# Mixer B's 24 attention tiles worked off inside the pair projections, with the three groups joined beside mixer M's keys and values

## The chip, the cores and the metric

One core of a Trainium2 chip runs the whole kernel. The metric is device time in microseconds (us) for one execution. Before the change the median of three runs is 1144.53 us (1140.45 to 1144.83).

## The reference

The kernel computes one layer of a causal decoder block on `x` (1024 tokens x 1024 channels) with a memory of 256 tokens. RMSNorm of `x` gives `h`; one projection of `h` is cut into the inputs of three mixers and three merge gates.

```python
h = RMSNorm(x)
# mixer A: chunked causal spatial gating:   u * (w_s @ layer_norm(v))
# mixer B: 3 groups x 4 heads (width 64), window attention at dilations 1, 4, 16
scores = einsum('bnqhd,bnkhd->bnhqk', qb, kb) * hd ** -0.5
scores = where(valid, scores + bias, -1e30)
m = max(scores);  p = exp(scores - m);  den = sum(p);  o = p @ v
# the three groups are then joined per token by weights exp(m_g - max_g m_g) * den_g
# mixer M: 4 heads (width 128) over the 256 memory tokens, softmax, values
# each mixer's output * silu(z), projected to 1024, times a sigmoid gate, summed
out = x + W_o @ merged
```

The queries and keys of B and M are normalised and scaled by learned weights; the rest of the reference has no bearing on the change.

## The kernel before, in words

All products run on TensorE (PE) with fp32 split into a high and a low part: `mm3` (L162 to L165) issues three matmuls, high x high, low x high and high x low. The program goes through these stages, one after the other on PE.

1. Load and norm of `x`, then mixer M's queries (`proj_mq`).
2. The "natural" products (tiles `n`, six blocks): B's queries and keys and its values, and A's value, with tokens on the partitions. They are stored to DRAM as `scr_qk[g]`, `scr_v[g]`, `scr_av`.
3. The pair projections (tiles `t`, the loop over `pairs` in `with ... as pp_`): everything that stays with channels on the partitions, that is A's `u` and gate (6 pairs), M's gate (2), B's gate (1) and the merge gates (12). Each of the 21 pairs is 7 Strassen-like products, and each product is 12 matmuls of 128x128 by 128x512 into a PSUM tile of tag "pj". `take` hands out the prepared left factor of a product; the steps in `steps` that prepare it (load raw weights, add them on VectorE (DVE), cast and subtract into `wh`/`wl`) run up to six factors ahead. `combine_products` adds the products up on DVE, `finish` applies Tanh or Gelu on ScalarE (ACT), and GpSimd (POOL) stores the two halves. In pairs 0 and 1 the memory `mem` is also loaded, squared, summed (`np_mem`) and normalised into `mh`, `ml` (`mem_steps`).
4. The attention stage. `kv_m` computes M's keys (`pk`, 48 matmuls) and values (`pv`, 48). `att_b` gives the steps of one of B's 24 tiles of 128 queries: `load` (queries and keys as tile `nat`, values as tile `v`, from DRAM), `s0` (four transposes into `qkt`, L765, copied out by ACT), `s1` (scores `sc`, plain at L799 for groups 1 and 2, three products for group 0; then add bias and take the maximum on DVE, L810; negate it, L812; Exp on ACT, L815), `s2` (four transposes per key block into `pt`, L823, copied out at L824) and `s3` (`po`, L830, copied at L836 and stored to `oscr` by POOL at L837). A tile has one key block or two: 13 have one, 11 have two. `att_m` does the same for the 8 tiles of M (`qt_m`, `sc_m`, `pr_m`, `pt_m`, `po_m`, with steps on POOL), and `combine` joins the three groups of B for 128 tokens (L851 to L897): mostly small steps on DVE, one transpose `yt` on PE.
5. `gates_b` and `gates` (tiles `pp`): the projections of the mixers' outputs, times the gates `tg` and `merged` that are loaded from `scr_g`.
6. The out projection (tiles `po`, `ro`).

The order of stage 4 is written by hand. `schedule` lays the steps of the tiles out by the lags in `LAGS`, `MLAGS` and `CLAGS`. The first nine rows of B's plan go into `queue`, and `spread(32)` with `pump()` pops them between the matmul triples of `kv_m`. Then B's steps continue with M's from `MSTART` on, two of B's to one of M's, with six rows of the combines mixed in from `CSTART` on. What is left of the combines is put in `queue` and popped between the first matmuls of `gates_b`. Engines run their own instructions in program order; DMA issues of SP and POOL are also in order on their queue.

Of the kernel before, what the change touches and what calls it, by code (L numbers as in the profile page):

```python
# [35 lines left out]


LAGS = (0, 2, 4, 6, 7)
MLAGS = (0, 1, 2, 4, 6, 8)
CLAGS = (0, 1, 2, 4)  # L40
MSTART = 9
CSTART = 22
CLATE = 30
# [3 lines left out]
def hybrid_block(  # L47
# [155 lines left out]
    def normalize(xs, pt, wcol, dst, cw, name, **kw):  # L203


        kp = KT // (cw // P)
# [207 lines left out]
    def load_raw(src, odd, name):  # L414
        if not odd:
            return raw(src, 512, name)
        st = tp.tile([P, 512], F32, name=f"wr_{name}", tag="wr", bufs=4)
        nc.sync.dma_start(out=st, in_=src)
        return st

    def prep_pair(i):
        add_steps([prepare_left(lambda q: load_raw(w_t[i][:, q * 512:(q + 1) * 512], i % 2, f"t{i}{q}"),
                                lambda: tp.tile([P, 512], F32, name=f"s1_{i}", tag="s1"), ready(f"t{i}"))])

    def prep_natural(b):
        add_steps([prepare_left(lambda q, kh=kh: load_raw(w_n[b, kh][:, q * 512:(q + 1) * 512], (b + (q in (1, 2))) % 2,
                                                          f"n{b}{kh}{q}"),
                                lambda kh=kh: (npool if kh else tp).tile([P, 512], F32, name=f"s1_n{b}{kh}", tag="s1"),
                                ready(f"n{b}{kh}")) for kh in range(2)])

    def combine_products(q, acc, sl, sa, sab, sc_, add):
# [7 lines left out]
        elif q == 3:  # L439
            V.tensor_tensor(out=sc_[:, sl], in0=acc, in1=sab[:, sl], op=ALU.add)  # L440
        elif q == 4:
            V.tensor_tensor(out=sab[:, sl], in0=acc, in1=sab[:, sl], op=ALU.add)
            add(3, acc, sc_[:, sl])
        elif q == 5:
            add(2, acc, sc_[:, sl])
# [11 lines left out]
    scr_b = [dram.tile([P, 4 * PW], F32, name=f"scr_b{g}") for g in range(3)]  # L457

    with tc.tile_pool(name="npool", bufs=1, side="right") as npool:
# [56 lines left out]
        for b, targets in enumerate(naturals):  # L516
            o = [rpool.tile([P, 2, 1024], F32, name=f"on{b}{c}", tag="r") for c in range(2)]
            sa, sab, sc_ = (npool.tile([P, 1024], F32, name=f"ns{c}{b}", tag=f"s{c}") for c in ("a", "ab", "c"))
# [46 lines left out]
            for q in range(7):  # L565
                w = take(2)
                rh, rl = rights[q]
                for t in range(2):
# [14 lines left out]
                    combine_products(q, acc, sl, sa, sab, sc_, add)  # L583
# [26 lines left out]
    with tc.tile_pool(name="ppool", bufs=1, side="right") as pp_:  # L610
# [5 lines left out]
        def finish(kind, o, q, name):  # L616

            d = o[q // 2][:, 512 * (q % 2):512 * (q % 2) + 512]
# [7 lines left out]
            if kind[0] == "u" and q in (1, 2):  # L626
                h = slice(512 * (q == 1), 512 * (q == 1) + 512)
                V.scalar_tensor_tensor(out=o[0][:, h], in0=o[1][:, h], scalar=0.5, in1=o[0][:, h],
                                       op0=ALU.mult, op1=ALU.mult)
# [3 lines left out]
        def mem_load(c):  # L633
            xm[c] = pp_.tile([P, KT, P], F32, name=f"xm{c}", tag="o", bufs=3)
            nc.sync.dma_start(out=xm[c], in_=memT[:, c * S:(c + 1) * S].rearrange("p (k t) -> p k t", t=P))

        def mem_squares(c):
            sm[c] = squares([xm[c]], P, f"mem{c}", G)

        def mem_norm(c):  # L640
            cs = slice(c * P, (c + 1) * P)
            normalize([xm[c]], sum_squares(sm[c], P, f"mem{c}"), mw,
                      lambda k0, xv: [(mh[:, k0:k0 + 4, cs], ml[:, k0:k0 + 4, cs], xv)], P, f"mem{c}", tag="rs")

        mem_steps = {(0, 0): [lambda: mem_load(0)], (0, 2): [lambda: mem_squares(0)],
                     (0, 4): [lambda: mem_norm(0), lambda: mem_load(1)], (0, 6): [lambda: mem_squares(1)],
                     (1, 0): [lambda: mem_norm(1)]}
        pages.append(pp_)
        mh, ml = (rpool.tile([P, KT, MEM], F32R, name=f"m{c}", tag="r") for c in "hl")
        for i, kind in enumerate(pairs):  # L650
            o = [pp_.tile([P, S], F32, name=f"o{i}{c}", tag="o", bufs=3) for c in range(2)]
            sa, sab, sc_ = (pp_.tile([P, 512], F32, name=f"s{c}{i}", tag=f"s{c}") for c in ("a", "ab", "c"))
            quarter = lambda q: o[q // 2][:, 512 * (q % 2):512 * (q % 2) + 512]

            def add(q, psum, s):
                V.tensor_tensor(out=quarter(q), in0=psum, in1=s, op=ALU.add)
# [12 lines left out]
            dst = {"u": lambda: [scr_us[kind[1]]],  # L669
                   "m": lambda: [scr_zm[2 * kind[1] + c] for c in range(2)],  # L670
                   "b": lambda: [scr_zb[c] for c in range(2)],
                   "g": lambda: scr_g[kind[1]][kind[2]:kind[2] + 2]}[kind[0]]()
            for c, t in enumerate(dst):
                G.dma_start(out=t, in_=o[c])
# [11 lines left out]
    oscr = {g: dram.tile([S, 264], F32, name=f"oscr{g}") for g in (1, 2)}  # L686
    cring = []

    def cb_(j):

        if not cring:
            cring.extend(rpool.tile([P, 2, 3, 264], F32, name=f"cring{i}", tag="r") for i in range(2))
        return cring[j // 2 % 2][:, j % 2]


    queue = deque()

    pace = [0.0, 0.0]

    def spread(slots):  # L700

        pace[0], pace[1] = len(queue) / slots, 0.0

    def drain():
        while queue:
            queue.popleft()()

    def pump():
        pace[1] += pace[0]
        while pace[1] > 0.999 and queue:  # L710
            queue.popleft()()
            pace[1] -= 1.0

    def schedule(tiles, lags):

        stages = [f() for f in tiles]
        return [[stages[t - lags[q]][q] for q in range(len(lags) - 1, -1, -1) if 0 <= t - lags[q] < len(tiles)]
                for t in range(len(tiles) + lags[-1])]

    def stream(tiles, lags):  # L720
        for step in schedule(tiles, lags):
            queue.extend(step)

    def rows(ap, g, j):


        d = DIL[g]
        if d == 1:
            return ap[j * P:(j + 1) * P, :]
        if d == 4:  # L730
            r, b = divmod(j, 2)
            return ap[512 * b:512 * (b + 1), :].rearrange("(i r) c -> r i c", r=4)[r]
        return ap.rearrange("(i r) c -> r i c", r=8)[j]

    def load_bias(g):
        b = ap_.tile([P, 4, 256], F32, name=f"bias{g}", tag="bias")
        c0 = 0 if g < 2 else 128
        v = bass.AP(scr_b[g].tensor, scr_b[g].offset + 127 + c0, [[4 * PW - 1, P], [PW, 4], [1, 256 - c0]])
        G.dma_start(out=b[:, :, c0:256], in_=v)
        return b  # L740

    def att_b(u, j):

        g = u.g
        nm = f"{g}{j}"
        split3 = g == 0
        kc = (j % 4) * P
        prev = (g == 0 and j > 0) or (g == 1 and j % 2 == 1)
        nk = 2 if prev else 1
        W = nk * P  # L750
        c = Unit()

        def load():
            if j == 0:
                u.bias = load_bias(g)
            c.nat = ap_.tile([P, 512], F32, name=f"nat_{nm}", tag="nat", bufs=3)
            nc.sync.dma_start(out=c.nat, in_=rows(scr_qk[g], g, j))
# [669 lines left out]
```

## Time and profile before

| | before |
|---|---|
| median of 3 runs | 1144.53 us |
| the profiled execution, its own time | 1145.57 us |
| its span from the first to the last instruction | 1143.9 us |
| PE busy | 1104.9 us (97% of the span) |
| DVE busy | 827.1 us (72%) |
| ACT busy | 490.6 us (43%) |
| POOL busy | 223.1 us (20%) |
| mean granted clock of PE | 0.982 of 2.4 GHz |

The stages stand in the span like this: natural products from 72.3 to 315.4 us, pair projections from 315.4 to 721.9, attention stage from 721.9 to 894.3, gates to 1064, out projection to the end. PE's busy time counts a matmul until its modelled end, and matmuls overlap, so the distance between the starts of two instructions tells more of what an instruction costs than its own duration does.

### The profile page before, as it was taken

To read this page: it belongs to the slowest core of one execution; us is meant where nothing else is said; L and a number is where in the kernel's file an instruction comes from. 1 tells how busy PE (TensorE), PEld (TensorE's weight loads), DVE (VectorE), ACT (ScalarE), POOL (GpSimd) and SP (SyncE) were. 2 spreads that over 40 slices of the span, in tenths; PEclk is the share of its full clock that TensorE was granted. 3 is DMA by queue.
4 is the path that set the end of the run, shared out by engine and by line. 5 is a ranking of instruction groups with operands and counts; after the bars stand their busy time and mean duration, and the time that the engine had idled before them with its cause. 6 is when DMAs were issued, how large, how long until landed. Compare 5 with 4: busy or idle time off the path is not lost. (4 is left out here: it accounts for less than half of the span.)

```text
span 1143.9 us, 18163 instructions
## 1 busy us (share of the span) xinstructions
PE 1104.9 (97%) x6664; PEld 966.1 (84%) x6664; DVE 827.1 (72%) x1741; ACT 490.6 (43%) x1031; POOL 223.1 (20%) x232
## 2 busy tenths in 40 slices
PE   8999999999999999999999999899999899998998
PEld 7789999999987888888888888677889677887998
DVE  6999899846888878775666664355899758559873
ACT  6653243223255434343434343457786373223320
POOL 0000441220000000000000000012332136656232
PEclk9999999999999999999999999898999899999899
DMA  6322322464232222332333314636433685522422
GB/s 194 109 82 89 121 94 94 140 220 131 96 122 88 92 94 91 109 123 96 110 111 114 108 74 138 206 114 179 134 93 89 226 283 184 177 97 65 138 101 85
DMA packets 75244, 143.33 MB, mean 125 GB/s; under 512 B 7973, under 2 KB 26004, under 8 KB 75156
## 3 DMA queue, kind: packets, MB, share of 16 engines
q1 hardware_dynamic: 63172, 101.59, 28.3%
q0 software_dynamic: 10544, 38.10, 9.3%
q10 hardware_dynamic: 1440, 2.49, 0.6%
q8 instruction: 52, 0.85, 0.3%
q14 instruction: 36, 0.29, 0.1%
HBM read 101.57 MB, written 42.94 MB: 126 GB/s over the span
## 5 line engine op out<-in xcount | busy, mean ns | idle before, releaser
L163 PE MATMUL t<-th,wh_t 128*128 128x512 f32 x336 | 132.5, 394 | 0.0
L165 PE MATMUL t<-th,wl_t 128*128 128x512 f32 x336 | 131.7, 392 | 0.0
L164 PE MATMUL t<-tl,wh_t 128*128 128x512 f32 x336 | 130.7, 389 | 0.0
L163 PE MATMUL n<-wh_n,th 128*128 128x256 f32 x384 | 108.2, 282 | 0.0
L165 PE MATMUL n<-wh_n,tl 128*128 128x256 f32 x384 | 107.6, 280 | 0.0
L164 PE MATMUL n<-wl_n,th 128*128 128x256 f32 x384 | 107.6, 280 | 0.0
L163 PE MATMUL t<-HH,wh_t 128*128 128x512 f32 x252 | 98.6, 391 | 0.0
L165 PE MATMUL t<-HH,wl_t 128*128 128x512 f32 x252 | 98.4, 390 | 0.0
L164 PE MATMUL t<-HL,wh_t 128*128 128x512 f32 x252 | 98.1, 389 | 0.0
L163 PE MATMUL n<-wh_n,HH 128*128 128x256 f32 x288 | 82.0, 285 | 0.0
L164 PE MATMUL n<-wl_n,HH 128*128 128x256 f32 x288 | 81.5, 283 | 0.0
L165 PE MATMUL n<-wh_n,HL 128*128 128x256 f32 x288 | 81.5, 283 | 0.0
L141 ACT CAST wh_t<-ws_t 128x512 fp32r<-128x512 f32 x66 | 40.8, 621 | 86.4 <-PE t L164 73.2
L165 PEld LDWEIGHTS t<-th,wl_t 128*128 128x128 f32 x336 | 63.1, 188 | 14.8
L164 PEld LDWEIGHTS t<-tl,wh_t 128*128 128x128 f32 x336 | 63.1, 188 | 14.0
L163 PEld LDWEIGHTS n<-wh_n,th 128*128 128x128 f32 x384 | 73.3, 191 | 1.5 <-issue 0.9
L163 PEld LDWEIGHTS t<-th,wh_t 128*128 128x128 f32 x336 | 63.2, 188 | 12.8
L164 PEld LDWEIGHTS n<-wl_n,th 128*128 128x128 f32 x384 | 72.1, 188 | 0.2 <-issue 0.2
L165 PEld LDWEIGHTS n<-wh_n,tl 128*128 128x128 f32 x384 | 72.2, 188 | 0.0
L141 ACT CAST wh_t<-wr_t 128x512 fp32r<-128x512 f32 x60 | 37.0, 621 | 77.5 <-PE t L164 70.5
L536 POOL TENSOR_TENSOR on<-on,nss 128x1024 f32<-128x1024 f32 x12 | 26.3, 2207 | 174.4 <-DVE nss L138 117.5
L165 PEld LDWEIGHTS t<-HH,wl_t 128*128 128x128 f32 x252 | 47.3, 188 | 10.4
(378 smaller groups left out, 3052.8 us busy)
## 6 DMA issues: line engine op xcount, KB each, us to landing
scr_g<-o POOLq DMA_DIRECT2D x24, 512.0 KB, 2.9
ws_t<-in_w_t SPq DMA_DIRECT2D x44, 256.0 KB, 3.0
wr_t<-in_w_t SPq DMA_DIRECT2D x40, 256.0 KB, 3.2
tg<-scr_g SPq DMA_DIRECT2D x16, 512.0 KB, 4.0
ws_n<-in_w_n SPq DMA_DIRECT2D x24, 256.0 KB, 3.1
wr_n<-in_w_n SPq DMA_DIRECT2D x24, 256.0 KB, 3.2
scr_qk<-on POOLq DMA_DIRECT2D x12, 512.0 KB, 4.4
nat<-scr_qk SPq DMA_DIRECT2D x24, 256.0 KB, 3.3
```

The costliest lines, as they stand in the source:

```text
L141: A.copy(out=hi, in_=y)
L163: T.matmul(o, lhsT=ah, rhs=bh, start=first, stop=False)
L164: T.matmul(o, lhsT=ah, rhs=bl, start=False, stop=False)
L165: T.matmul(o, lhsT=al, rhs=bh, start=False, stop=last)
L536: G.tensor_tensor(out=v, in0=v, in1=ss[:, 16 * ORD[q]:16 * ORD[q] + 16].unsqueeze(2) .to_broadcast([P, 16, 64]), op=ALU.mult)
```

## The change

- B's 24 tiles move from stage 4 into the pair projections. `start_b` writes their steps into `queue` (98 entries: `first`, `s2`, `s1`, `last` for each tile, in the order of groups 2, 1, 0), and `spread(7*(PAIRS-2)-1)` spreads them over 132 products: `pump()` after each product pops 0.74 of a step on average. `drain()` stands after the last pair.
- The tiles' buffers come from elsewhere: keys (`bk`), bias and `nat` (both in `bx`) from the ring of big tiles `rpool`, `pr` and `pT` from the rings of prepared weights `wh` and `wl` (9 each), scores from PSUM tag "sc" (2 banks) in place of "pj". All copies `pT` and `ob` are ACT's. The factors are prepared 5 ahead in place of 6.
- All three groups' outputs go to `oscr` in DRAM (24 stores in place of 16), and a combine loads three pieces in place of two.
- The pair stage gives up a buffer (`sc_`), its output tiles are 512 wide with a store for each, and some raw weights of odd pairs use other buffers.
- The memory's load, squares and norm move from pairs 0 and 1 to pairs 19 and 20, with 32 matmuls of the squares' sums in place of 16.
- Stage 4 has `kv_m` with the combines in `queue` (`spread(40)`: 32 slots in `kv_m`, the rest after the rows of M's plan), then M's 8 tiles by themselves. Nothing of the attention is left for `gates_b`'s queue if the 40 slots take it all.

```diff
+        for t in range(n + 1):
+            queue.append(lambda t=t: first(t))
+            if t:
+                queue.append(lambda t=t: tiles[t - 1].s2())
+            if t < n:
+                queue.append(lambda t=t: tiles[t].s1())
+            queue.append(lambda t=t: last(t))
...
+        start_b()
+        spread(7 * (PAIRS - 2) - 1)
         for i, kind in enumerate(pairs):
...
-                (lh, ll), = take(1)
+                (lh, ll), = take(1, 5)
...
-                combine_products(q, acc, slice(0, 512), sa, sab, sc_, add)
+                combine_products(q, acc, slice(0, 512), sa, sab, add)
+                pump()
                 for f in mem_steps.get((i, q), ()):
                     f()
...
+        mem_steps = {(PAIRS - 2, 4): [lambda: mem_load(0)], (PAIRS - 2, 6): [lambda: mem_squares(0)],
+                     (PAIRS - 1, 1): [lambda: mem_norm(0)], (PAIRS - 1, 2): [lambda: mem_load(1)],
+                     (PAIRS - 1, 4): [lambda: mem_squares(1)], (PAIRS - 1, 6): [lambda: mem_norm(1)]}
...
     rsqrt(mss, 32, 1.0 / 128)
-    bs = schedule([(lambda g=g, j=j: att_b(ug[g], j)) for g in (2, 1, 0) for j in range(8)], LAGS)
-    for t in range(MSTART):
-        queue.extend(bs[t])
-    spread(32)
+    stream([(lambda j=j: combine(j)) for j in range(8)], CLAGS)
+    spread(40)
     kv_m()
...
+    for step in schedule([(lambda j=j: att_m(j)) for j in range(8)], MLAGS):
+        for f in step:
             f()
+        pump()
     spread(12)
```

The rows below are the program's instructions in the order of one engine, out<-in and shape. The first place is PE in the first pair, between the second product (`t_1`) and the fourth (`t_3`). Before:

```order
L164 MATMUL t_1_3822<-HL,wh_t_2_3601 128x512
L165 MATMUL t_1_3822<-HH,wl_t_2_3602 128x512
L163 MATMUL t_2_3841<-th_117,wh_t_6_3675 128x512
L164 MATMUL t_2_3841<-tl_121,wh_t_6_3675 128x512
L165 MATMUL t_2_3841<-th_117,wl_t_6_3676 128x512
...
L163 MATMUL t_3_3864<-th_118,wh_t_7_3679 128x512
```

And now:

```order
L159 MATMUL t_1_3805<-HH,wl_t_2_3599 128x512
L524 MATMUL qkt_3821<-ident,bx 128x128 x4
L157 MATMUL t_2_3843<-th_117,wh_t_6_3672 128x512
L158 MATMUL t_2_3843<-tl_121,wh_t_6_3672 128x512
...
L159 MATMUL t_2_3843<-th_117,wl_t_6_3673 128x512
L554 MATMUL sc_3861<-bk_3775,qh_3826 128x128
L554 MATMUL sc_3862<-bk_3775,qh_3826 128x128
L554 MATMUL sc_3861<-bk_3775,qh_3826 128x128
L554 MATMUL sc_3862<-bk_3775,qh_3826 128x128
L157 MATMUL t_3_3881<-th_118,wh_t_7_3676 128x512
```

The first tile's transposes (`qkt`) and scores (`sc`) now stand between whole products of 12 matmuls, one product apart.

The second place is ACT at the same point of the first pair: `wh_t` are the casts of weights, `o` the activations of a finished quarter, `sa` a copied product. Before:

```order
L434 COPY sa_3782<-t_0_3793 128x512
L141 CAST wh_t_7_3926<-wr_t_3818 128x512
L623 ACTIVATE o_3780<-o_3780 128x512
L186 ACTIVATE xq_mem_3855<-xm_3807 128x512
L186 ACTIVATE xq_mem_3857<-xm_3807 128x512
L141 CAST wh_t_5_3948<-s_1_3878 128x512
```

And now:

```order
L537 ACTIVATE qh_3826<-qkt_3821,wq_87 128x256
L803 ACTIVATE o_3818<-o_3818 128x512
L538 ACTIVATE bk_3775<-qkt_3821,colt 128x2x128
L135 CAST wh_t_1_3877<-wr_t_3835 128x512
L570 ACT_TABLE_LOAD
L570 ACTIVATE pr_3857,ob_3859<-pr_3857,ng_3860 128x128 x2
L570 ACTIVATE pr_3858,ob_3859<-pr_3858,ng_3860 128x128 x2
L135 CAST wh_t_2_3895<-wr_t_3837 128x512
L135 CAST wh_t_6_3924<-wr_t_3835 128x512
```

The tile's copies and its four Exp (L570, line 815 before) stand among the casts of weights, behind a load of a function table; over the whole program ACT has 23 such loads where it had 9.

The third place is SP's queue of loads beside the products of M's keys and values: `ws_kvv` are the raw weights of the values, `cb` and `cring` the pieces for a combine. Before:

```order
L146 DMA ws_kvv_7312<-in_w_kv 128x512
L146 DMA ws_kvv_7318<-in_w_kv 128x512
L757 DMA nat_7120<-scr_qk_652 128x512
L759 DMA v_7122<-scr_v_655 128x256
L757 DMA nat_7127<-scr_qk_652 128x512
```

And now:

```order
L140 DMA ws_kvv_8660<-in_w_kv 128x512
L1090 DMA merged_9496<-scr_g_679 128x512
L1090 DMA merged_9497<-scr_g_680 128x512
L888 DMA cb_8487<-oscr_702 128x264
L891 DMA cb_8487<-oscr_703 128x1x264
L892 DMA cb_8487<-oscr_704 128x1x264
...
L892 DMA cb_8544<-oscr_704 128x1x264
L140 DMA ws_kvv_8666<-in_w_kv 128x512
```

Nine pieces for the first three combines and five loads of gates (`merged`) now stand ahead of the last five of M's eight value weights; the loads of B's `nat` and `v` are gone from here.

## Rows read from the trace of the kernel before

**Rows 1.** Busy time by stretch: from:to, us, PE, PEld, DVE, ACT, POOL, clock, DMA share, GB/s.

```profile
315.40:721.90 406.50, 405.63 (x1783) 333.01 (x1782) 278.77 (x470) 171.72 (x269) 22.06 (x38) 1.00 0.31 105
721.90:767.00 45.10, 40.83 (x205) 31.23 (x204) 20.30 (x85) 22.05 (x67) 5.25 (x7) 0.85 0.52 165
721.90:894.30 172.40, 158.91 (x1186) 137.31 (x1185) 125.33 (x507) 118.32 (x395) 44.37 (x53) 0.93 0.45 135
894.30:904.60 10.30, 6.44 (x34) 5.08 (x32) 7.27 (x22) 3.13 (x9) 0.76 (x1) 0.95 0.61 177
904.60:990.00 85.40, 81.51 (x416) 66.12 (x417) 58.10 (x80) 35.44 (x79) 40.33 (x28) 0.97 0.73 238
```

**Rows 2.** Timeline of PE in 721.9 to 767: start us, us, instruction, out<-in, count.

```profile
750.52 0.60 PE L765 MATMUL qkt<-ident,nat 128*128 128x128 f32 x4
...
751.19 0.40 PE L164 MATMUL pv<-wl_kvv,mh 128*128 128x512 f32 x1
...
752.35 1.00 PE L830 MATMUL po<-v,pT 128*128 128x64 f32 x8
...
753.48 0.39 PE L164 MATMUL pv<-wl_kvv,mh 128*128 128x512 f32 x1
...
754.65 0.60 PE L823 MATMUL pt<-ident,pr 128*128 128x128 f32 x4
...
755.33 0.39 PE L164 MATMUL pv<-wl_kvv,mh 128*128 128x512 f32 x1
755.56 0.40 PE L165 MATMUL pv<-wh_kvv,ml 128*128 128x512 f32 x1
...
756.87 0.39 PE L164 MATMUL pv<-wl_kvv,mh 128*128 128x512 f32 x1
```

**Rows 3.** Timeline of PE where tiles of group 0 run, two key blocks each.

```profile
821.00 1.04 PE L823 MATMUL pt<-ident,pr 128*128 128x128 f32 x8
821.97 0.39 PE L163 MATMUL sc<-kh,qh 64*128 64x256 f32 x2
...
822.88 0.66 PE L765 MATMUL qkt<-ident,nat 128*128 128x128 f32 x4
...
826.44 1.90 PE L830 MATMUL po<-v,pT 128*128 128x64 f32 x16
828.18 0.61 PE L823 MATMUL pt<-ident,pr 128*128 128x128 f32 x4
```

**Rows 4.** Busy time of one tile's instructions by engine, 721.9 to 894.3: `pr`, `ob`, `qkt`, `pt`.

```profile
721.90:894.30 172.40, 21.59 (x140) 16.84 (x140) 29.92 (x96) 44.80 (x192) 0.93 0.45 135
721.90:894.30 172.40, 25.54 (x168) 9.02 (x16) 0.93 0.45 135
721.90:894.30 172.40, 17.80 (x96) 11.97 (x96) 7.22 (x16) 20.20 (x48) 0.93 0.45 135
721.90:894.30 172.40, 21.59 (x140) 16.84 (x140) 8.23 (x12) 12.77 (x23) 0.93 0.45 135
```

**Rows 5.** Groups of instructions on ACT: loads of function tables, mean ns.

```profile
L613 ACT ACT_TABLE_LOAD x2 | 2.6, 1283 | 3.6 <-DVE o L656 3.6
```

**Rows 6.** Busy time of the tile `sc_m` on PE, PEld, DVE and ACT, 721.9 to 894.3.

```profile
721.90:894.30 172.40, 15.15 (x96) 13.15 (x96) 10.68 (x16) 15.75 (x64) 0.93 0.45 135
```

**Rows 7.** Timeline of PE at the end of M's tiles and the start of the gates.

```profile
890.80 3.74 PE L1008 MATMUL po_m<-pT_m,mv 128*128 128x128 f32 x32
894.29 0.48 PE L163 MATMUL pp<-yb0h,wh_p 128*128 128x512 f32 x1
...
904.57 0.77 PE L163 MATMUL pp<-yb0h,wh_p 128*128 128x512 f32 x1 [3.86 <-DVE merged L1097]
...
910.60 0.39 PE L165 MATMUL pp<-yb0h,wl_p 128*128 128x512 f32 x1
```

**Rows 8.** Waits of PE in 721.9 to 912: waited for, us, times, longest.

```profile
PE pp L163 <- DVE merged L1097: 3.9, 1, 3.9
...
PE pt L823 <- ACT pr L815: 2.0, 1, 2.0
```

More of the change, by code (lines that the diff above doesn't have):

```diff
@@ L457, in hybrid_block, with spread, drain, pump @@
     scr_b = [dram.tile([P, 4 * PW], F32, name=f"scr_b{g}") for g in range(3)]
+    oscr = [dram.tile([S, 264], F32, name=f"oscr{g}") for g in range(3)]
+    queue = deque()
+    pace = [0.0, 0.0]
+    def spread(slots):
+        pace[0], pace[1] = len(queue) / slots, 0.0
+    def drain():
+        while queue:
+            queue.popleft()()
+    def pump():
+        pace[1] += pace[0]
+        while pace[1] > 0.999 and queue:
+            queue.popleft()()
+            pace[1] -= 1.0
+    def schedule(tiles, lags):
+        stages = [f() for f in tiles]
+        return [[stages[t - lags[q]][q] for q in range(len(lags) - 1, -1, -1) if 0 <= t - lags[q] < len(tiles)]
+                for t in range(len(tiles) + lags[-1])]
@@ new lines, in hybrid_block, with keys, start_b, first @@
+    mb = Unit()
+    def keys(g):
+        k = rpool.tile([P, 2, 2, 512], F32R, name=f"bk{g}", tag="r")
+        mb.kh, mb.kl = k[:, 0], k[:, 1]
+    def start_b():
+        keys(2)
+        bx = rpool.tile([P, 4, 512], F32, name="bx", tag="r")
+        mb.bias = bx[:, 0:2, :].rearrange("p a (b t) -> p (a b) t", t=256)
+        mb.nat = bx[:, 2:4, :]
+        tiles = []
+        for g in (2, 1, 0):
+            u = Unit()
+            u.g, u.v = g, []
+            tiles += [att_b(u, j) for j in range(8)]
+        n = len(tiles)
+        tiles[0].load_bias()
+        tiles[0].load_nat()
+        tiles[0].load_v()
+        def first(t):
+            if t == 16:
+                keys(0)
+            if t < n:
+                tiles[t].s0()
+            if t + 1 < n:
+                tiles[t + 1].load_nat()
+        def last(t):
+            if t + 1 < n and (t + 1) % 8 == 0:
+                tiles[t + 1].load_bias()
+            if t:
+                tiles[t - 1].s3()
+            if t + 1 < n:
+                tiles[t + 1].load_v()
+        for t in range(n + 1):
+            queue.append(lambda t=t: first(t))
+            if t:
+                queue.append(lambda t=t: tiles[t - 1].s2())
+            if t < n:
+                queue.append(lambda t=t: tiles[t].s1())
+            queue.append(lambda t=t: last(t))
@@ L637, in mem_squares @@
+            for k in range(2):
+                nc.sync.dma_start(out=xm[c][k], in_=memT[:, c * S + 512 * k:c * S + 512 * k + 512]
+                                  .rearrange("p (k t) -> p k t", t=P))
         def mem_squares(c):
[L638 removed]
+            sm[c] = squares(xm[c], P, f"mem{c}", V, 0)
         def mem_norm(c):
+            if not mem:
+                mem.extend(rpool.tile([P, KT, MEM], F32R, name=f"m{c}", tag="r") for c in "hl")
             cs = slice(c * P, (c + 1) * P)
[L642 to L643 removed]
@@ L665, in hybrid_block @@
                     mm3(acc, lh[:, c], ll[:, c], rh[:, kk, :], rl[:, kk, :], kk == 0, kk == 3)
-                combine_products(q, acc, slice(0, 512), sa, sab, sc_, add)
+                combine_products(q, acc, slice(0, 512), sa, sab, add)
+                pump()
                 for f in mem_steps.get((i, q), ()):
                     f()
[L669 to L674, printed above, removed]
+        drain()
+        mh, ml = mem
         pages.pop()
@@ L685, in hybrid_block @@
     ap_ = att.enter_context(tc.tile_pool(name="att", bufs=2, side="right"))
[L686 to L733, printed above, removed]
```

278 lines of the change are left out of this document (133 added, 145 removed).

## The prediction, made before the changed kernel ran

> **What bounds the kernel now.** I read three views in this order: the busy time by stretch, PE's timeline inside the stretches, and PE's waits. In the first the reader should compare two rows [rows 1]. The pair projections take 406.5 us, and PE is busy 405.63 of them at a granted clock of 1.00: nothing is late there, the stage is as long as its matmuls. DVE is busy 278.8 us of it, ACT 171.7, POOL 22. The attention stage from 721.9 to 894.3 is another case: 172.4 us, a clock of 0.93, and DVE and ACT at 73% and 69%. There every tile is a chain over three engines, and PE waits or runs slowly between the links. So the change takes work out of a stretch where it is badly packed and puts it into one whose only limit is PE, and which has time left on DVE and ACT. A step there costs what it adds to PE's queue and no more, as long as its inputs are ready.
>
> **Part 1: 24 tiles between the products.** The price of a step between 128x512 matmuls can be read where the kernel already does it, among M's value products [rows 2]. Two matmuls without anything between them start 0.23 us apart (755.33, 755.56). From the start of a step to the start of the second matmul behind it, less one such pitch, I get: `qkt` 750.52 to 751.19, 0.44; `po` 752.35 to 753.48, 0.90; `pt` 754.65 to 755.33, 0.45; `sc` 755.56 to 756.87 less two pitches, 0.85. One tile with one key block: 2.64 us. With two key blocks I take the tile of group 0 [rows 3]: `pt` 0.97 (821.00 to 821.97), `sc` 0.91, `po` 1.74 (826.44 to 828.18), and `qkt` 0.44 as before, and 0.1 for the pitch that is lost behind a step: 4.2 us. Of the 13 single-block tiles one is split in three products and I count it with the dear ones: 12 x 2.64 + 12 x 4.2 = **82 us**. The steps' own durations would give more, but they overlap.
>
> Is the cover there? DVE gets the additions with the maximum (29.9 us, tile `pr`), the small steps on `ob` (up to 25.5, of which the copies go to ACT) and the low parts (7.2): at most 63 us. ACT gets the Exp (44.8), the copies of `qkt` (20.2), 35 copies of `pt` at 12.77 / 23 = 0.56 (19.4) and 24 copies of `po`, which I put at 10: 94 us [rows 4]. (In the row of `ob` the two columns are DVE and POOL.) Over 488 us of stage that makes DVE (279 + 63) / 488 = 70% and ACT (172 + 94 + 18) / 488 = 58%. The 18 us are 14 more loads of function tables, Exp against Gelu, at 1.283 us [rows 5]. None of it ends a product later unless it comes in a heap. From a tile's scores to its `pt` there are three steps, some four products or 11 us of PE; a tile's Exp chain is 4 to 6 us by the same rows.
>
> The Trainium skill, page "ScalarE: Activation LUTs", section "What ACT_TABLE_LOAD costs", puts each switch at about 2.66 us, because a drain of 1.38 us stands beside the load, and the page's rule is to batch calls by table set, which this change breaks. By that figure ACT would have 37 us in place of 18, an estimate that leaves it at 62%; no row here shows the drain.
>
> The loads `nat`, `v` and the bias and the 24 stores have their data long before they are wanted, and the stores of the pair stage double in number at half the size; SP and POOL have little else to do there. I cost them at nothing; POOL's 22 us are the cover. The memory's norm in pairs 19 and 20 is moved, and costs 16 more small matmuls: 16 x 0.11 (a quarter of a `pt`) = 1.8 us. So the last product ends at 721.9 + 82 + 1.8 = **805.7**, bounds 800 (single steps cheaper than their distance) and 815 (some 0.4 us of wait for each tile).
>
> **Part 2: what is left of the attention stage.** M's keys and values are 96 x 0.23 = 22.1 us on PE, and 24 transposes for `kt` and `yt` are 2.6: 24.7. They can't run that fast. The norm of the memory's second half now ends with the last product and not 380 us before it: Sqrt with a table load, a reciprocal and the split into `mh`, `ml`, about 2 us before the first `pk`. And SP now has the nine pieces of the combines and five gate loads ahead of the last five value weights. Some 5.6 MB must come in this time (weights 1.3 to 2.6, gates 1.3 to 1.8, pieces 1.2 to 2), and at the 238 GB/s of the busiest stretch [rows 1] that is 24 us. Loads and matmuls would each take 24 to 25 us; in sequence for a part of the way I take 34, with the 2 us 36.
>
> M's eight tiles then stand alone. A tile costs PE 0.45 for `qt_m`, 0.97 for two `pt_m`, at most 15.15 / 8 = 1.9 for `sc_m` [rows 6] and (894.29 - 890.80) / 2 = 1.75 for `po_m` [rows 7]: 5.1, or 40 us for all. No other tile fills PE in the first and last steps of the plan, where one tile's chain runs through ACT, DVE and POOL: 6 us more, three hand-overs of 2 us, the size of the wait for `pr` [rows 8]. 46, and 2 for the combines in it: **48 us**. The gates would start at 805.7 + 36 + 48 = 889.7, bounds 876 (kv 27, M 43) and 905 (kv 42, M 57). They started at 894.3: **-4.6**.
>
> **Part 3: the gates.** The first projections (`pp`) ran from 894.29, then PE waited 3.86 us at 904.57 for `merged`, and the next 14 matmuls took 6.03 us, 0.43 each in place of 0.23, which is the lower of the clock's two levels, 1.2 GHz: 2.8 us lost [rows 7, 8]. With 0.8 for the transposes between them that is 7.5 us that need not come again, since the first gates are now loaded before M's tiles and no combine is left. I take **-5**, because A's part behind them can wait for DVE as before; bounds 0 and -7.5.
>
> **Sum.** -4.6 - 5 = -9.6 on the profiled execution's 1145.57 us: 1136. The median of the runs is 1.0 lower than that execution, so **1135 us**. The out projection and the rest of the gates are untouched.
>
> **Rivals.** (a) *The gain is lost in M's stage.* 82 us of matmuls that were mixed with M's are gone from it; M's 5 us bursts stand between chains. For it: the stretch 721.9 to 767, where PE waited for B's first loads, has a clock of 0.85, and after the one wait of 3.86 us PE ran at 1.2 GHz [rows 1, 7]. If half of M's 40 us ran at that level, 40 x 0.5 = 20 us would be at half speed, so 10 more than in the sum: 1145, no change. Against it: M's DVE and ACT parts are smaller than its PE part, so PE may keep busy. The Trainium skill, page "TensorE: Matmul & The Clock Gate", section "HAM oscillation — how this bites in real kernels", tells of bursts of matmuls with waits between them that fall back to the lower clock each time; the trace agrees, with the 14 matmuls at 0.43 us. 0.22.
>
> (b) *Slower: PE waits at each tile's steps in the pair stage.* The place is PE's queue at `pt` (and `po`), which waits for Exp, which is in order on ACT behind casts of weights, table loads and what DVE brings late. PE's queue is in order too: behind a late `pt` stands the next product. One such wait was 2.0 us in the old stage [rows 8]. It decides from 15 us in all, 0.63 us for each tile; at 1 us a tile the kernel takes 1135 + 24 = 1159. Against it: four products lie between scores and `pt`, and PE's idle time in the stage was 0.9 us of 406.5 [rows 1]. 0.12; with other late links (the tail's loads) I give the slower side 0.14.
>
> (c) *The tail packs well*: kv 30, M 44, all of part 3: 805.7 + 74 = 879.7, -14.6 - 7.5 = -22: 1123. Half of that gain, 1128, is the more probable end. 0.19.
>
> (d) *The steps don't go where the text says*, the scheduler moving them behind the pairs: the order of PE shows `qkt` and `sc` between the first products, so I give it nothing.
>
> **Chances.** The forecast 0.45, (a) 0.22, (b) and its like 0.14, (c) 0.19. A measurement of this kernel can tell about 0.5%, 5.7 us, from no change. Faster than 1138.8: nearly all of (c), and 0.85 of the forecast, and a little of (a): 0.58. Within: the rest of the forecast and most of (a): 0.27. Slower than 1150.3: 0.15. The range leaves out the far half of (b) and the far end of (c): 1124 to 1150.
>
> **What would show it.** Right: the pair stage 406 + 84 = about 490 us with PE above 98% busy and a clock of 1.00, DVE near 70%; the first `pp` near 890; no wait for `merged`. Step by step: the distance from product to product with a `po` between 0.9 or 1.8 longer; `pk` starting 2 us after the last product; M's part 44 to 50 us. Wrong: idle PE before `pt` in the pair stage that names ACT (b), a clock below 0.9 in M's part (a), or PE waiting for `wl_kvv` for more than 12 us.

## The result and the profile after

The changed kernel takes 1156.66 us (median of 4 runs, 1154.61 to 1159.64), the kernel before beside it 1142.49 (4 runs). The ratio is 1.013, with a 95% interval of 1.0089 to 1.017: slower by 1.3%, clear of noise, where 1135 and a range of 1124 to 1150 were forecast. The table sets the two profiled executions side by side, by the starts of the first instruction of a tile on PE.

| stage | before, us | after, us | difference | forecast |
|---|---|---|---|---|
| start to the first `n` | 72.5 | 73.1 | +0.6 | 0 |
| natural products | 243.0 | 247.5 | **+4.4** | 0 |
| first `t` to the last product | 406.2 | 488.4 | +82.2 | +83.8 |
| last product to the first `pk` | 0.2 | 1.9 | +1.7 | +2 |
| the tail: first `pk` to the first `pp` | 172.3 | 96.9 | **-75.4** | -90.3 |
| first `pp` to the last `pp` | 156.4 | 152.7 | -3.7 | -5 |
| out projection | 88.9 | 88.9 | 0 | 0 |
| PE's last instruction to the end | 4.3 | 8.1 | **+3.8** | 0 |
| span | 1143.9 | 1157.6 | +13.7 | -9.6 |

The busy time by stretch of the kernel after has the columns of [rows 1]:

```profile
73.10:320.60 247.50, 245.01 (x2028) 240.91 (x2027) 193.70 (x378) 79.33 (x131) 50.26 (x49) 0.99 0.37 123
320.60:809.20 488.60, 488.60 (x2535) 402.14 (x2534) 309.28 (x712) 265.88 (x576) 53.78 (x98) 1.00 0.35 114
809.20:907.80 98.60, 76.10 (x456) 64.66 (x455) 84.98 (x239) 51.44 (x142) 35.01 (x35) 0.88 0.59 182
...
810.90:825.00 14.10, 12.51 (x52) 9.03 (x51) 8.89 (x22) 7.74 (x12) 0.54 (x1) 1.00 0.86 277
825.00:845.00 20.00, 13.98 (x54) 10.12 (x53) 17.76 (x72) 5.15 (x12) 4.28 (x6) 0.91 0.86 265
845.00:870.00 25.00, 14.66 (x78) 12.26 (x78) 24.00 (x66) 8.57 (x23) 13.03 (x13) 0.71 0.74 229
870.00:890.00 20.00, 18.21 (x133) 17.31 (x134) 19.23 (x47) 15.89 (x52) 10.38 (x10) 0.85 0.14 40
```

Read the second row first. With 24 tiles among its products PE is busy in all of the pair stage, at full clock, and DVE is at 309 / 489 = 63%, ACT at 54%. The third row is another kind of stretch: PE 77% and clock 0.88. Its cut into pieces says who holds it: from 825 to 890 DVE is busy 61.0 of 65 us, and from 845 to 870 it has 1 us free while PE has 10. The forecast counted this stage in loads and matmuls; the engine with the least to spare in it is DVE.

The price of a step in the pair stage can be read where the forecast read it in [rows 2], on PE's timeline of the kernel after:

```profile
480.76 0.40 PE L159 MATMUL t<-HH,wl_t 128*128 128x512 f32 x1
481.00 0.60 PE L578 MATMUL pt<-ident,pr 128*128 128x128 f32 x4
481.35 0.48 PE L157 MATMUL t<-HH,wh_t 128*128 128x512 f32 x1
481.67 0.39 PE L158 MATMUL t<-HL,wh_t 128*128 128x512 f32 x1
...
843.21 0.39 PE L159 MATMUL pv<-wh_kvv,ml 128*128 128x512 f32 x1
846.10 0.66 PE L959 MATMUL kt<-ident,knat 128*128 128x128 f32 x4 [2.50 <-POOL knat L978]
848.06 0.41 PE L925 MATMUL yt<-ident,cb 128*128 128x128 f32 x2 [1.31 <-issue]
848.84 1.09 PE L959 MATMUL kt<-ident,knat 128*128 128x128 f32 x4 [0.37 <-DVE mx L901]
854.36 0.66 PE L925 MATMUL yt<-ident,cb 128*128 128x128 f32 x2 [4.43 <-DVE mx L907]
854.82 1.49 PE L1003 MATMUL qt_m<-ident,mnat 128*128 128x128 f32 x6
```

A `pt` costs 481.67 - 481.00 - 0.23 = 0.44 us, against 0.45 forecast. The second half of the fence is the place where PE stood longest in the tail. The last value product starts at 843.21 and M's first step, `qt_m`, at 854.82: 11.6 us with 12 transposes of 128x128 in it. The longest wait is not for anything of M's. It is that of a combine's transpose `yt`, which stands ahead of `qt_m` in PE's order and waits 4.43 us for DVE. DVE's timeline of the same us shows why:

```profile
844.54 1.79 DVE L916 TENSOR_TENSOR cb<-cb,ew 128x256 f32<-128x256 f32 x2
846.25 1.26 DVE L919 TENSOR_TENSOR cb<-cb 128x256 f32<-128x256 f32 x1
...
847.54 0.42 DVE L920 TENSOR_TENSOR cb<-cb 128x256 f32<-128x256 f32 x1
...
847.95 0.74 DVE L963 SCALAR_TENSOR_TENSOR mkl<-kt,colt,mkh 128x512 fp32r<-128x512 f32 x1
...
849.81 1.20 DVE L136 TENSOR_TENSOR yb0l<-cb,yb0h 128x256 fp32r<-128x256 f32 x1
...
851.01 0.74 DVE L963 SCALAR_TENSOR_TENSOR mkl<-kt,colt,mkh 128x512 fp32r<-128x512 f32 x1
851.68 0.78 DVE L916 TENSOR_TENSOR cb<-cb,ew 128x256 f32<-128x256 f32 x2
852.38 0.41 DVE L919 TENSOR_TENSOR cb<-cb 128x256 f32<-128x256 f32 x1
...
852.83 1.28 DVE L920 TENSOR_TENSOR cb<-cb 128x256 f32<-128x256 f32 x1
```

Lines 916 to 920 are sums of combines, and only the two `mkl` belong to M's keys. DVE isn't idle between these rows: 24.00 of 25 us. The waits of PE from 809 to 908 name what it was short of (us, times, longest):

```profile
PE yt L925 <- DVE mx L907: 4.4, 1, 4.4
PE pt_m L1036 <- POOL pr_m L1027: 3.2, 5, 1.6
PE pv L158 <- DVE wl_kvv L136: 2.7, 1, 2.7
PE kt L959 <- POOL knat L978: 2.5, 1, 2.5
PE pt_m L1036 <- ACT pT_m L1037: 2.3, 2, 1.8
```

None names a load, but the DMA share of 0.86 shows the loads to be close, and ACT's casts `wh_kvv`, from which `wl_kvv` is made, waited 2.7 us for theirs. In the gates the 3.9 us wait for `merged` [rows 8] is gone, and the first `pp` follow each other at 0.23 us.

### The profile page after: what moved, and what is told of

Its sections match the earlier page's. It is cut to its first block, busy times and chain, and to the rows that moved or that the text cites. A ratio compares the mean times of both kernels' runs of the same rounds, so it can differ in the third digit from the quotient of the medians.

```text
span 1157.6 us, 18260 instructions
## 1 busy us (share of the span) xinstructions
PE 1105.1 (95%) x6680; PEld 963.2 (83%) x6680; DVE 807.1 (70%) x1697; ACT 515.5 (45%) x1081; POOL 242.9 (21%) x274
## 5 line engine op out<-in xcount | busy, mean ns | idle before, releaser
L157 PE MATMUL t<-th,wh_t 128*128 128x512 f32 x336 | 137.0, 408 | 0.0
L157 PE MATMUL t<-HH,wh_t 128*128 128x512 f32 x252 | 102.5, 407 | 0.0
L849 DVE TENSOR_TENSOR o<-t,sa 128x512 f32<-128x512 f32 x63 | 43.3, 688 | 39.5 <-PE t L159 21.2
L815 POOL DMA_DIRECT2D scr_g<-o x48 | 26.0, 542 | 207.5 <-ACT o L801 172.4
L135 ACT CAST wh_t<-ws_t 128x512 fp32r<-128x512 f32 x86 | 52.1, 619 | 34.4 <-PE t L158 18.2
L136 DVE TENSOR_TENSOR wl_t<-ws_t,wh_t 128x512 fp32r<-128x512 f32 x86 | 58.2, 686 | 9.1 <-ACT wh_t L135 8.7
```

What stands on the lines that cost most here:

```text
L135: A.copy(out=hi, in_=y)
L136: (eng or V).tensor_tensor(out=lo, in0=y, in1=hi.bitcast(F32), op=ALU.subtract)
L157: T.matmul(o, lhsT=ah, rhs=bh, start=first, stop=False)
L815: G.dma_start(out=t[:, h], in_=d)
L849: V.tensor_tensor(out=o[q], in0=psum, in1=s, op=ALU.add)
```

## The experiments

All names of stages are those of the table. In some of these kernels the first `pp` starts ahead of M's last `po_m`, so tails are compared by **first `pk` to last `pp`**: 328.8 us before, 249.6 after, 82 + 151.4 = 233.4 by the forecast. Four kernels whose tail isn't edited (e1_raws, e5_nat, e6_act, e11_nat4) give 247.3 to 250.4 with 249.6 among them: differences up to 3 us are not told by such a number.

### Combines held back (e2_late), and half held back (e3_pv, e7_even)

```diff
-    stream([(lambda j=j: combine(j)) for j in range(8)], CLAGS)
-    spread(40)
     kv_m()
+    stream([(lambda j=j: combine(j)) for j in range(8)], CLAGS)
+    spread(16)
```

> The changed kernel with the eight combines queued behind mixer M's keys and values, two steps after each row of M's plan, and none between the key and value products. Theory D (the tail from the last pair product to the gates, 98.6 us, is bound by DVE, which is busy 85 of it, 41 with the combines): keys and values end some 12 us earlier, but the combines' DVE work then lies on M's tiles, so that the tail is 86 to 92, gain 6 to 12 us. Rival L (the value weights' loads stood behind the combines' pieces on SP): the tail loses the whole of the 10 us of waits before M's first tile and M's 53 us stay: 84 to 87. Rival C (M's tiles alone run at the lower clock for want of matmuls): M's part stays 53 or grows, no more than 3 us gained.

e3_pv keeps the queue but pops it only between the value products, so that most of the value weights are loaded ahead of the combines' pieces; e7_even pops it more slowly:

```diff
 e3_pv
-                pump()
+                if name == "pv":
+                    pump()
-    spread(40)
+    spread(24)
 e7_even
-    spread(40)
+    spread(48)
```

> The changed kernel with the combines' steps popped only between the value products, not between the key products (24 slots in place of 40), so that the value weights' loads come ahead of most of the combines' pieces on SP. Theory D: the same DVE work in a shorter stretch, tail 95 to 102 as before (98.6). Rival L: PE's waits for wl_kvv and wh_kvv (3.8 us and the half clock after them) go, tail 88 to 93.

> The changed kernel with the combines' steps a fifth thinner: 48 slots in place of 40, so that about 21 of the 32 steps lie in the keys and values and 11 in M's tiles (26 and 6 before; 0 and 32 gave a tail of 83.0, 24 slots in the values alone gave 99.0). Theory D in its form after those runs (the small steps of the combines stand ahead of the keys', values' and M's own links in DVE's queue; the fewer stand there, the shorter): tail 89 to 95 in place of 96.9. Rival (DVE's total work sets the tail): unchanged, 96 to 98.

Measured: e2_late 1150.64 us, 1.007 [1.0046, 1.0094]; e3_pv 1161.21, 1.016 [1.0131, 1.0189]; e7_even 1158.89 in its one run, which tells no more than that it isn't much faster.

### The combines' sums left out (e4_nosums)

Here the weighting and adding of the three groups is left out, 32 instructions on DVE and 8 on POOL; B's output is then group 0's alone, unweighted.

```diff
-            for g in range(3):
-                o4 = cb[:, g, 0:256].rearrange("p (h d) -> p h d", d=64)
...
-            V.tensor_tensor(out=ys, in0=ys, in1=cb[:, 2, 0:256], op=ALU.add)
+            pass
```

> The changed kernel with the combines' weighted sums left out (sums() of combine: three products with the weights and two additions for 128 tokens, 8 times; mixer B's output is then group 0's alone, unweighted). The loads, the weights' small steps, the transposes and the splits stay. Theory D: DVE loses some 18 us and POOL 5.5, and what waits behind them goes too: tail 80 to 88 in place of 98.6. Rivals L and C: tail 95 or more, since the loads and M's tiles are the same.

Measured: 1148.29 us in one run. The five kernels together, with the combines' work that lies before M's first `qt_m` (busy time on DVE without the splits into `yb`; transposes `yt` on PE):

| | DVE us of combines before `qt_m` | `yt` matmuls before it | first `pk` to `qt_m` | first `pk` to last `pp` |
|---|---|---|---|---|
| after | 21.2 | 10 | 43.9 | 249.6 |
| e3_pv | 15.7 | 8 | 41.4 | 250.0 |
| e7_even | 17.0 | 8 | 38.0 | 245.8 |
| e2_late | 9.8 | 0 | 32.0 | 240.6 |
| e4_nosums | 11.1 | 10 | 36.3 | 237.6 |

The keys and values are shorter where less of the combines' DVE time stands before `qt_m`, though not in strict proportion. e2_late takes 11.4 us of it out of the way and `qt_m` starts 12 us sooner; but with the DVE steps it also moves the combines' loads and the `yt` in PE's order. e4_nosums leaves those where they were, takes only 10.1 us of work out, and gains 7.6. e3_pv shows what doesn't help, the loads' order: the last value weight is issued at 825.4 us in place of 836.1, and PE's waits for `wl_kvv` and `wh_kvv` fall from 3.8 us to 0.2, but its waits at `yt` rise from 8.2 to 12.4 and the total stays. So the rival of the loads (L) named a real wait that was not worth anything by itself. Of the expected tails, which were counted from the end of the last product, e3_pv with 100.7 lies in D's range and outside L's; e4_nosums with 88.2 lies just above D's 88, far from the 95 of L and C. In e2_late the work isn't gone, it comes later, beside M's tiles: the whole stretch gains 9.0, inside D's 6 to 12, and in the stretch from the end of the products DVE is as full as before, while PE's longest waits there are for POOL. Its busy time by stretch (columns of [rows 1]):

```profile
809.50:893.00 83.50, 68.04 (x428) 57.35 (x427) 71.12 (x210) 49.19 (x136) 33.39 (x34) 0.96 0.64 204
...
842.50:870.00 27.50, 20.89 (x163) 18.38 (x161) 25.20 (x74) 19.44 (x60) 17.19 (x17) 1.00 0.69 226
```

The granted clock rose from 0.88 to 0.96 although nothing was done for it; from 842.5 to 870, where `after` had 0.71 in its own 845 to 870, it is 1.00. So the low clock was here a consequence of PE's waits more than a cause of its own. M's part did not become shorter with the higher clock: from `qt_m` to the last `po_m` it takes 54.6 us at 0.97, in `after` 53.0 at 0.87, and 50.2 at 0.93 without sums.

### The natural products (e1_raws, e5_nat, e11_nat4)

After the change PE waits in the first natural block, and a stretch at 1.2 GHz follows (87.4 to 90.8 us). The waits of the kernel after, 73 to 320 us:

```profile
PE n L158 <- DVE wl_n L136: 1.4, 1, 1.4
PE n L157 <- ACT wh_n L135: 1.1, 1, 1.1
```

On SP's queue (start, us from the first issue to the end of the last, count) the loads behind these weights start late. The kernel before, then the kernel after:

```profile
72.59 1.80 SPq L418 DMA_DIRECT2D wr_n<-in_w_n  x4
```

```profile
73.55 0.80 SPq L412 DMA_DIRECT2D wr_t<-in_w_t  x2
78.05 2.60 SPq L412 DMA_DIRECT2D wr_n<-in_w_n  x4
```

(`wr_t` are two raw weights of pair 1, which are loaded as early as this because their buffers are free; they take SP 0.8 us.) SP's wait in front of 78.05 is 3.6 us, for `scr_q<-qnat`, the last stores of M's queries. The kernel before has the same wait, 3.3 us, but behind the four `wr_n`, in front of `oh`, which is there the first load into that pool. e1_raws moves the new tiles to other addresses inside their pool, away from the memory that `qnat` had; e5_nat puts two of block 0's four displaced tiles in an older pool; e11_nat4 puts all four in older pools.

```diff
 e1_raws
+        first_s = [npool.tile([P, 1024], F32, name=f"ns{c}0", tag=f"s{c}") for c in ("a", "ab")]
...
 e5_nat
+                      *((tp, 2) if (b, kh) == (0, 0) and q in (1, 2) else
+                        (npool if (b + (q in (1, 2))) % 2 else None, 4)),
 e11_nat4
+                      *(((tp, 2, "wr"), (wpool, 9, "wh"))[kh] if b == 0 and q in (1, 2) else
+                        (npool if (b + (q in (1, 2))) % 2 else None, 4, "wr")),
```

> The changed kernel with one thing other: the buffers nsa and nsab of the natural products are taken first in their pool, so that the four early raw-weight tiles wr_n no longer lie where the qnat and qjk tiles of mixer M's queries lay. In the changed kernel their loads were issued at 78.1 us against 72.6 before, and PE lost 1.1 and 1.4 us waiting at 86 and then ran at 1.2 GHz from 87.4 to 90.8. Theory (the buffer's place delays the loads): the natural products take 243 us again in place of 247.5, so the whole is 4 to 5 us shorter than the changed kernel, near 1152. Rival (the loads were late for the queue or the smaller look-ahead): unchanged, 1156 to 1157.

> The changed kernel with two of the four early raw-weight tiles of the first natural block in pool tp, where all four lay before, and two in npool. Moving the tiles inside npool had left their loads at 77.4 us and the natural products at 247.8. Theory (npool as a whole is opened on memory that the last store of mixer M's queries still reads, and its first load waits for that, tp does not): two loads are issued at 72.6 again, the waits at 86 us and the 1.2 GHz stretch behind them go, naturals 243 to 245, the whole 3 to 5 us under the changed kernel. Rival (it is the order on SP, two pair weights ahead of them): unchanged, 247 to 248.

> The changed kernel with none of the four early raw tiles in npool: two in tp, two in the ring wh. Two in npool gave naturals of 246.4 and four 247.5. Theory (npool's first load waits for the last store of mixer M's queries): all four loads at 72.6 us, no wait of PE near 86 us, no 1.2 GHz stretch there, naturals 243.0 to 243.5. Rival (the order on SP or the look-ahead): 246 or more.

Measured for the natural stage: e1_raws 247.8 us (1158.44, 1.0148 [1.0114, 1.0181]), e5_nat 246.4 (1154.95, 1.0098 [1.0066, 1.013]), e11_nat4 243.0 (1154.69 in one run). The address isn't what counts: my first reading fell with e1_raws, where SP still waits 3.9 us for `scr_q<-qnat` in front of a tile that lies elsewhere. e5_nat's 246.4 is between the two ranges that were expected: its two loads in the older pool are issued at 72.57, the two others still at 77.65. In this program the first load into a pool opened on memory that is still being stored from waits, at every place in the pool that was tried, and the cost ends when block 0 uses no tile of that pool. In e11_nat4 PE has no wait at all in the stage. Block 0's four loads are the first row and the three of the second; the wait, 3.8 us, now stands behind them, in front of block 1's four, where it costs PE nothing:

```profile
17.92 0.42 SPq L412 DMA_DIRECT2D wr_n<-in_w_n  x1
...
68.49 4.34 SPq L412 DMA_DIRECT2D wr_n<-in_w_n  x3
...
76.74 1.75 SPq L412 DMA_DIRECT2D wr_n<-in_w_n  x4
```

### The stores on ACT's queue (e6_act)

```diff
-            G.dma_start(out=oscr[g][j * P:(j + 1) * P, :], in_=c.ob)
+            A.dma_start(out=oscr[g][j * P:(j + 1) * P, :], in_=c.ob)
...
-            G.dma_start(out=t[:, h], in_=d)
+            (A if kind[0] == "g" else G).dma_start(out=t[:, h], in_=d)
```

> The changed kernel with 72 stores issued by ACT and not by POOL: the gates' 48 of the pair stage and mixer B's 24 of oscr. POOL then issues 52 DMAs; it issued 80 before and 124 in the changed kernel, and its drain at the end of the program took 4.38 us before and 8.22 us in each of the five runs with 124. Theory (the drain grows with the number of DMAs that POOL issued): under 4 us, and the time from PE's last matmul to the end falls from 8.1 to 3.7 to 4.4 us, where SP's last store ends; gain 4 us if the issues on ACT delay nothing. Rival (the end is longer for another reason, the longer program): 8.1 stays.

Measured: 1153.68 us, 1.0084 [1.0054, 1.0114]. At the program's end every engine has closing instructions, and POOL has three drains among them. The first is the long one; when it is over, some 0.8 us of closing are left. The third figure is its length in ns, in the kernel after and in e6_act (the view of the last line of the program):

```profile
L1443 POOLq DRAIN  x3: 45/102/8217, 1148.5 to 1157.3; - x3
```

```profile
L1443 POOLq DRAIN  x3: 45/102/2581, 1148.3 to 1153.0; - x3
```

After has 132 DMAs issued by POOL, before 88 and e6_act 60 (the counts of the expectation are 8 too small); the drain takes 8.22, 4.38 and 2.58 us. From PE's last instruction to the end it is 8.1, 4.3 and 4.1: with 60 DMAs POOL's drain is over at 1150.9, and it is SP's wait for its last store, until 1151.5, that ends the program. From the first `t` to the first `pk` it stays at 490.3 us with 72 more DMA issues on ACT.

### The memory's norm one pair earlier (e10_mem)

```diff
-        mem_steps = {(PAIRS - 2, 4): [lambda: mem_load(0)], ...
+        mem_steps = {(PAIRS - 3, 4): [lambda: mem_load(0)], ...
...
-        spread(7 * (PAIRS - 2) - 1)
+        spread(7 * (PAIRS - 3) - 1)
```

> The changed kernel with the memory's load, squares and norm one pair earlier and mixer B's steps spread over 125 products. The changed kernel waited 1.7 us between the last product and the first pk. Expected: that wait goes and the tail is 95 to 96 from the first pk; the combines' place is unchanged, so no more than 3 us are gained. If the late norm was what held the tail back, 88 or less.

Measured: 1160.92 us in one run. The wait before `pk` (1.7 us) is gone, and last product to last `pp` is 246.5 in place of 251.6; but the pair stage grew by 2.9 us, to 491.3, so 2.2 are left, less than such a number tells. The start and the natural stage, which the edit doesn't touch, were 3.8 us longer in this execution, so nothing can be read from its total.

### All together (e8_all, e9_best)

e8_all is e2_late, e5_nat and e6_act in one; e9_best is e2_late, e6_act, e10_mem and e11_nat4.

> The three together: combines behind the keys and values, two early raw tiles in tp, 72 stores on ACT. If each holds by itself and they add up: pair stage 490, tail 83, gates 157, naturals 244, end 4: 7 + 4 + 4 us under the changed kernel, 1141 to 1143, level with the kernel before. If ACT's stores delay PE in the pair stage: pair stage above 492 and 1145 or more.

> Combines behind the keys and values and 72 stores on ACT, as in the run of all three, with two further edits: none of the four early raw tiles lies in npool (two in tp, two in the ring wh), and the memory's load, squares and norm stand one pair earlier, with mixer B's steps spread over 125 products in place of 132. Expected if the parts hold: naturals 243.0 (245.1 in the run of all three), no wait of PE for mh at the first pk (3.4 us and a 1.2 GHz stretch of 3.4 us there), pair stage 490 or a little over, tail 76 to 79 in place of 81.6, end 4: 1136 to 1140, 0.4 to 0.8% under the kernel before. Rival: the 24 tiles and the norm now crowd DVE in the pair stage, which grows beyond 493: 1142 to 1146.

Measured: e8_all 1145.13 us, 1.0005 [0.9987, 1.0023]; e9_best 1142.70, 0.999 [0.9971, 1.0009], 12 runs each. The corrections add up: 1.013 less 0.006, 0.0032 and 0.0046 is 0.999, and e8_all, 2 us above the 1141 to 1143 expected of it, has 1.0005. e9_best has the natural stage at 243.0, the end at 4.1 and 240.7 from the first `pk` to the last `pp`, and is level with the kernel before. The 1136 to 1140 that were expected of it were missed in the tail: 82.5 us to the first `pp`, where 76 to 79 were expected, with the pair stage at 490.4 as expected.

### POOL's scaling moved to ACT (e12_prn)

What was left in e9_best are M's tiles, 55.6 us from `qt_m` to the last `po_m`; PE's longest wait there is for POOL's scaling of `pr_m`. So this step goes to ACT, on top of e9_best:

```diff
-                G.tensor_tensor(out=c.pr[hp], in0=c.pr[hp], in1=s.unsqueeze(2).to_broadcast([P, 2, 256]), op=ALU.mult)
+                for e in range(2):
+                    A.activation(out=c.pr[hp][:, e, :], in_=c.pr[hp][:, e, :], func=AF.Copy, scale=s[:, e:e + 1])
```

> The version with all corrections, and one thing other: the scaling of mixer M's probabilities pr_m by their sums runs on ACT (four activations of 256 columns for each tile) and not on POOL (two products of 512, 1.09 us each), whose result PE waited for at pt_m: 3.7 us in that version, 5.5 where the combines were only moved. ACT has 37 us of work in M's 55.6 us there, DVE 51. Theory (M's tiles stay near 55 us, where 48 were forecast, because the chain over POOL is late and POOL's work slows DVE's): M's part 48 to 52, whole 1137 to 1140. Rival (DVE, 92% busy there, or ACT with 13 us more holds it): 54 to 57 and 1142 to 1145.

Measured: 1143.76 us, 0.9998 [0.9974, 1.0021]: no gain, and M's tiles take 59.0, beyond the rival's 54 to 57 too. The waits of PE from 837 to 893 us, in e9_best and then in e12_prn:

```profile
PE pt_m L1037 <- POOL pr_m L1028: 3.7, 4, 2.2
PE sc_m L157 <- ACT qh_m L1006: 2.3, 2, 1.5
```

```profile
PE sc_m L157 <- ACT qh_m L1006: 6.2, 5, 2.3
PE pt_m L1038 <- ACT pT_m L1039: 4.2, 2, 3.6
```

POOL's wait is gone, and ACT took its place with more than it. The busy times of M's tiles in each, from the first `qt_m` to the last `po_m` (columns of [rows 1]), first e9_best:

```profile
837.50:893.10 55.60, 46.39 (x339) 42.34 (x340) 51.25 (x146) 37.09 (x119) 27.11 (x27) 0.94 0.54 165
```

```profile
838.50:897.40 58.90, 47.25 (x335) 43.52 (x336) 45.32 (x145) 49.34 (x149) 9.80 (x11) 0.91 0.50 153
```

ACT rose by 12.3 us, to 49.3 of 58.9; DVE fell by 5.9 us with 145 instructions in place of 146, although the edit takes nothing from it. DVE's total did not hold M's tiles in e12_prn, then: it has more to spare, and they take longer.

## Why the prediction was wrong

**Part 1 held**, in its mechanism too: 82.2 us measured for 83.8, and the price of a `pt` as read. There is no wait of PE in the stage, so rival (b) fell: it had named the right direction of the result and the wrong place. The 17 table loads between Exp and Gelu cost PE nothing. Their groups in the kernel after (busy us, mean ns, idle us ahead of them):

```profile
L570 ACT ACT_TABLE_LOAD x9 | 11.5, 1283 | 8.7 <-issue 8.6
L803 ACT ACT_TABLE_LOAD x8 | 10.3, 1283 | 0.1
```

The Trainium skill, page "ScalarE: Activation LUTs", section "What ACT_TABLE_LOAD costs", gives the load the same 1283 ns; its drain of 1.38 us a switch is not seen here: of the 17 loads 15 start within 0.02 us of the end of ACT's instruction before them, and the 8.7 us at L570 are two stretches of 5.4 and 3.2 us in which ACT stood without work.

**Part 2 failed**, and by itself it turns the sign: 24.7 us of PE and "24 us" of loads for the keys and values, "46, and 2 for the combines in it" for M's tiles. (8 x 5.1 is 41 and not 40, a small slip.) Both counts are of PE, of hand-overs and of the DMAs; no term is of DVE's work. Two things were left out. The eight combines are about 40 us on DVE, not 2 us of PE; their largest groups on DVE from 809 to 908, in the kernel after:

```profile
L916 DVE TENSOR_TENSOR cb<-cb,ew 128x256 f32<-128x256 f32 x16 | 9.6, 636 | 0.0
...
L920 DVE TENSOR_TENSOR cb<-cb 128x256 f32<-128x256 f32 x8 | 4.5, 562 | 0.0
L919 DVE TENSOR_TENSOR cb<-cb 128x256 f32<-128x256 f32 x8 | 4.1, 516 | 0.0
...
L930 DVE SCALAR_TENSOR_TENSOR cb<-zb,yt 128x256 f32<-128x256 f32 x8 | 3.3, 410 | 0.5 <-PE yt L925 0.5
```

The fourteen groups of the combines come to 40.3 us; the rest are splits into `yb` (5.7) and steps on 4 or 12 columns. And they stand, in order, ahead of the next link of the keys, the values and M's tiles. DVE's part could have been had in advance. DVE was busy 125.3 us in the old attention stage [rows 1], and part 1 itself moved "at most 63 us" of it away. At least 62 us of 82 had to remain, in a stage in which the forecast gave DVE no place. An upper bound of what moves is careful for the stage that receives it and hopeful for the one that gives: DVE's busy time in the pair stage rose by 309.3 - 278.8 = 30.5 us only, and measured in the tail are 85.0 of 98.6. The keys and values took 43.9 us in place of 34, M's tiles 53.0 in place of 48: the 14.9 us by which the tail missed. e2_late shows the first part: hold the combines back, and it takes 32.0. The second is bounded but not settled: M's tiles stay between 50.2 and 59.0 us in every kernel, whether POOL or ACT scales, and without the sums too. Which of their chains over DVE, ACT and POOL would have to go for 48 I can't say.

**Rival (a)** described a real thing, the tail's clock of 0.88, with the wrong cause. It put the waits to M's own chains and gave 10 us (by its own rows, 0.43 for 0.23, 20 us of work at the lower level would cost some 17 more); the deepest fall, 0.71, stands where PE waits for a combine, and in e2_late, where that wait is gone, the clock came back. What the forecast held against (a), that M's DVE part is smaller than its PE part, left the combines out: from 854.8 to 907.8 DVE is busy 47.5 us and PE 45.3. The Trainium skill, page "TensorE: Matmul & The Clock Gate", section "HAM oscillation — how this bites in real kernels", tells of such a fall between bursts; the trace agrees with the 0.71 of 845 to 870, where PE is idle 10 of 25 us.

**Part 3** held: -3.7 for -5. The wait for `merged` is gone; A's waits for DVE (`mx` for `mt`) grew from 2.5 to 6.3 us, which is what the forecast had kept 2.5 us back for. Rival (c) fell with part 2.

**Two terms were missing.** The loads and stores: "I cost them at nothing; POOL's 22 us are the cover". The cover was real and the price was elsewhere, 3.8 us in POOL's drain at the end (e6_act). And "some raw weights of odd pairs use other buffers" is one clause of the change; that with it those of the natural blocks moved to the natural stage's own pool is not said there, and none of it was given a price: 4.4 us in the natural stage (e11_nat4), through a pool that opens on memory still in use. Without these two terms `after` would still have been about 5 us slower.

**Where the gain went.** In e9_best, with both mended and the combines late, the pair stage and the wait behind it take 84.2 us more than before, and first `pk` to last `pp` 88.1 less. B's tiles cost in the pair stage nearly what they free in the tail; 4 us of gain in this comparison is near the limit of what the runs tell, and the ratio of 0.999 includes no change. Combines among the pair products were not tried.

## What to carry to other kernels

When work is moved out of a mixed stretch, add up for every engine what remains there, not only what leaves: each engine's busy time in the stretch, less what moves, is a lower bound of what is left, and the largest of them is a lower bound of the new stage. Here it was 62 us, under the forecast of 82, so it would not have refuted the forecast; it would have named the engine that the sum lacked. Work it out with the least that may move as well as with the most. Small steps that nobody is waiting for go behind the links of the longest chain on an engine that works in order, not ahead of them, even if there seems to be room: here that gave 9 of 249.6 us. Price also where a change puts buffers and stores: the first load into a pool that opens on busy memory, and what an engine's many DMAs cost at the program's end.

## What the runs showed of the hardware

- POOL's long drain at the program's end grew with the number of its DMAs: 60, 88 and 132 gave 2.58, 4.38 and 8.22 us.
- DVE instructions with two inputs in SBUF take two or three times as long at some places: L919 0.41 and 1.26 us, L920 0.42 and 1.28, both in the fence of DVE's timeline above. The long ones stand beside work on POOL: of the 16 instructions of these two lines in the kernel after, nine run without POOL and take 0.41 to 0.43, and of the seven beside an instruction of POOL three take 0.74 to 1.28, the other four 0.40 to 0.42. POOL's timeline of the kernel after:

```profile
844.82 2.40 POOL L978 TENSOR_TENSOR knat<-knat,kss 128x512 f32<-128x512 f32 x2
...
852.78 1.04 POOL L998 TENSOR_TENSOR mnat<-mnat,mss 128x512 f32<-128x512 f32 x1 [0.94 <-DMA mnat<-scr_q]
```

  L919 at 846.25 and L920 at 852.83 run beside them, L920 at 847.54 and L919 at 852.38 do not. In e12_prn, with 17 us less on POOL, the splits `ym00l` and `yb0l` fall from 643 to 418 and from 651 to 414 ns against e9_best. The Trainium skill, page "GPSIMD Engine Reference", section "1. Specifications", says that POOL shares its SBUF interfaces with VectorE and contends with DVE instructions that have two SBUF inputs; the trace agrees, with these sizes. No run isolated it by itself, so the share of the 14.9 us that it makes is open.
